# A two-layer decoder trunk on one core: a hand-written ScalarE order at three seams, weight casts placed behind the last turned block, and a different order inside a turned block

## The chip, the cores and the metric

The kernel runs on one core of one Trainium2 chip. The metric is device microseconds (us) of one execution, the median of several runs. The engines are named as the profile names them: PE is the matrix engine and PEld its weight loads, DVE is VectorE, ACT is ScalarE, POOL is GpSimd, SP is the engine that issues most of the DMAs. Results of PE land in eight PSUM banks, called `banks` in the rows; everything else lies in SBUF.

## The reference, cut to what matters

The trunk has a retention layer, then a native-sparse-attention (NSA) layer, and each is followed by a SwiGLU FFN. Every sub-layer is wrapped in two RMS norms: its output is normalised and added to the stream `h`, and the sum is normalised again on its way into the next sub-layer.

```
def rms_norm(x, g):
    y = x * rsqrt(mean(x * x, axis=-1) + 1e-6)
    return y * g
def swiglu_ffn(x, w_in, w_out):
    gate, up = split(x @ w_in, 2)
    return (silu(gate) * up) @ w_out
# x: 512 tokens of 1024 values, float32
h = h + rms_norm(sublayer(rms_norm(h, g_pre)), g_post)      # four times
```

The place where one sub-layer ends and the next begins is called a **seam** here: the last product of the one, both norms, and the first products of the next. There are three: A (retention to FFN 0, near 395 to 456 us), B (FFN 0 to NSA, near 765 to 829 us) and C (NSA to FFN 1, near 1085 to 1151 us).

## The kernel before

**Products.** Float32 accuracy is made from three products of a reduced type: `mm3` (lines 246 to 251) multiplies high by high (L249), high by low (L250) and low by high (L251), for operands that stand as a pair of a rounded high part and the rest. A weight tile is fetched by a DMA that SP issues (L225) into one of three `raw` buffers, ACT makes its high part (L237), and DVE subtracts that from the raw tile to make the low part (L240). Regular weights go through two buffers of each part (`whi`, `wlo`); weights that are kept for longer lie in slots of a pool and read `r` in the rows.

**A seam.** `out_stage` computes the sub-layer's output with tokens on the partitions, in two halves of 512 columns and four blocks of 128 tokens. `evac` takes a bank: ACT squares it with a running sum (L417), DVE multiplies it by the gain row (L418). `norm` (L345 to L364) serves one half of the tokens, p = 0 or 1: DVE makes an inverse root in a chain of small steps from L354 on, adds to `h` (L358), ACT squares with a sum (L359), DVE makes the second root, and the result is scaled into `t`, one block by ACT (L363), one by DVE (L364). Then the tokens must lie along the free axis again: `turn(p, kp)` transposes four 128x128 pieces on PE into one bank (L373), and for each of its two k ACT writes the high part (L376) and DVE the low part (L377). At seam B, where the turned stream is also wanted in plain form, ACT copies each of the two (L383).

**Products inside the seam.** `lead` fetches six weight tiles of the next sub-layer ahead of time. `prods` multiplies them with the first half of the tokens while the second half is still being normed, and `rest` with the second half once it is turned. `low(j)` is the DVE step for the low part of such a tile. So PE goes through these steps: the last product of the sub-layer, with the transposes of the first half in the middle of it; 144 products of 256 columns (six tiles, eight k, three each) with three more blocks of transposes among them; then four blocks of transposes of the second half and again 144 products of 256 columns; then the next sub-layer's regular products of 512 columns.

**What sets the order.** The program's order within an engine is chosen by a scheduler, except within a block where it is fixed by hand as the code is written:

```
with self.tc.manual_schedule(engines={E.PE, E.DVE}):
```

In `out_stage` that covers PE and DVE; ACT's place for each cast and each high part is the scheduler's. `more()` fetches as many of the six tiles as the pool has room for, whenever it is called. The NSA stage runs by a planner's list with its own `stream` of weights (high part at L1228, low part at L1232).

## Time and profile before

| what | value |
| --- | --- |
| median of three runs | 1488.17 us (1487.72 to 1488.86) |
| the profiled execution, own time | 1486.86 us |
| its span in the trace | 1485.1 us |
| PE busy | 1459.6 us, 98% of the span |
| ACT busy | 600.6 us, 40% |
| DVE busy | 732.1 us, 49% |
| granted PE clock, mean | 0.998 of full speed |

The profiled execution takes 1.76 us more than its span, and 1.31 us less than the median of the runs. Matrix products are pipelined in the trace, so that the next one starts before the end of the one ahead of it is shown: the distance from start to start is what a product costs, and a bracket behind a row gives the time the engine stood idle ahead of that row and the engine and tile that released it.

### The profile page before, as it was taken

Reading aid. Unit: us, or ns where it says so; the run is one execution under the profiler, and the core shown is the slowest. Engines: PE = TensorE matmul, PEld = TensorE weight load, DVE = VectorE, ACT = ScalarE, POOL = GpSimd, SP = SyncE. Lnnn points to the kernel's source line nnn. Section 1 sums busy time; section 2 is a strip of 40 time slices with the busy share of each in tenths; the row PEclk is TensorE's granted clock in tenths of the full one; section 3 lists DMA queues with packets and bytes.
Section 4 is the critical chain, followed back from the end, with each engine's and each line's share of the span. In section 5 each row is a group of like instructions: output and inputs, shape, how many; then the busy total and the mean of one; then the engine's idle time right before and its main releaser. Section 6 shows DMA issues by size and latency. Waiting matters only on the chain.

```text
span 1485.1 us, 18650 instructions
## 1 busy us (share of the span) xinstructions
PE 1459.6 (98%) x7286; PEld 1232.6 (83%) x7286; DVE 732.1 (49%) x1315; ACT 600.6 (40%) x1050; POOL 249.9 (17%) x369
## 2 busy tenths in 40 slices
PE   8999999999999999999998999999999999999997
PEld 6888888888888888888887988888889888888886
DVE  7546464734463333332346637888755333333244
ACT  5334333333442332222236348988753233322130
POOL 1012130402000000000000748787300000000000
PEclk9999999999999999999999999999999999999999
DMA  5223222325332344332243351321331222333231
GB/s 209 71 78 98 80 86 78 100 74 171 115 99 86 119 134 140 117 99 97 96 150 119 114 176 51 93 82 48 100 100 58 84 91 95 114 99 99 95 119 57
DMA packets 47833, 151.87 MB, mean 102 GB/s; under 512 B 5744, under 2 KB 6384, under 8 KB 47744
## 3 DMA queue, kind: packets, MB, share of 16 engines
q1 hardware_dynamic: 46560, 147.47, 31.2%
q10 hardware_dynamic: 1152, 3.15, 0.6%
q8 instruction: 57, 0.93, 0.3%
q14 instruction: 32, 0.26, 0.1%
q0 software_dynamic: 32, 0.07, 0.0%
HBM read 141.22 MB, written 9.44 MB: 101 GB/s over the span
## 4 chain that ended last, share of the span: by engine, by line
PE 92%; DVE 4%; DMA 2%; ACT 2%; issue 1%; SPq 0%; DVEq 0%; ACTq 0%
PE banks L250 27%; PE banks L249 27%; PE banks L251 27%; PE banks L1533 2%; PE banks L1555 1%; PE banks L1467 1%; PE banks L1468 1%; PE banks L1554 1%; DMA raw<-in_ffn_w_in_dram 1%; PE banks L1046 1%; DMA raw<-in_kv_w_n_dram 1%; DVE r L240 1%; PE banks L1365 1%; DVE r L1544 0%; ACT f L359 0%
## 5 line engine op out<-in xcount | busy, mean ns | idle before, releaser
L237 ACT ACTIVATE whi<-raw 128x1024 fp32r<-128x1024 f32 x165 | 174.7, 1059 | 518.8 <-PE banks L250 335.8
L249 PE MATMUL banks<-r,whi 128*128 128x512 f32 x912 | 357.4, 392 | 0.0
L251 PE MATMUL banks<-r,wlo 128*128 128x512 f32 x912 | 356.4, 391 | 0.0
L250 PE MATMUL banks<-r,whi 128*128 128x512 f32 x912 | 355.3, 390 | 0.0
L240 DVE TENSOR_TENSOR wlo<-raw,whi 128x1024 fp32r<-128x1024 f32 x165 | 206.0, 1249 | 299.2 <-ACT whi L237 295.2
L250 PE MATMUL banks<-r 128*128 128x256 f32 (+2 forms) x600 | 198.4, 334 | 5.0 <-DVE r L377 4.2
L250 PE MATMUL banks<-wlo,r 128*128 128x512 f32 x520 | 202.9, 390 | 0.0
L251 PE MATMUL banks<-whi,r 128*128 128x512 f32 x520 | 202.6, 390 | 0.0
L249 PE MATMUL banks<-r 128*128 128x256 f32 (+2 forms) x600 | 194.4, 333 | 8.0 <-ACT r L208 5.7
L251 PEld LDWEIGHTS banks<-r,wlo 128*128 128x128 f32 x912 | 171.2, 188 | 36.3 <-DVE f L678 0.7
L249 PEld LDWEIGHTS banks<-r,whi 128*128 128x128 f32 x912 | 171.3, 188 | 34.8 <-issue 0.9
L250 PEld LDWEIGHTS banks<-r,whi 128*128 128x128 f32 x912 | 171.3, 188 | 34.3
L251 PE MATMUL banks<-r 128*128 128x256 f32 (+2 forms) x600 | 195.3, 329 | 0.0
L249 PE MATMUL banks<-whi,r 128*128 128x512 f32 x520 | 178.5, 390 | 0.0
L250 PEld LDWEIGHTS banks<-r 128*128 128x128 f32 x600 | 114.1, 190 | 18.7 <-DVE r L377 8.0
L249 PEld LDWEIGHTS banks<-r 128*128 128x128 f32 x600 | 112.0, 191 | 20.7 <-ACT r L208 5.7
L251 PEld LDWEIGHTS banks<-r 128*128 128x128 f32 x600 | 114.2, 191 | 10.1 <-DVE r L209 0.2
L251 PEld LDWEIGHTS banks<-whi,r 128*128 128x128 f32 x520 | 97.6, 188 | 20.3 <-issue 0.2
L250 PEld LDWEIGHTS banks<-wlo,r 128*128 128x128 f32 x520 | 97.7, 188 | 20.2 <-issue 0.2
L249 PEld LDWEIGHTS banks<-whi,r 128*128 128x128 f32 x520 | 97.7, 188 | 20.0
L575 DVE TENSOR_TENSOR f<-banks,f 128x512 f32<-128x512 f32 x44 | 30.4, 692 | 137.7 <-PE banks L251 133.5
L949 POOL TENSOR_TENSOR r<-f,r 64x512 fp32r<-64x512 f32 x8 | 10.9, 1366 | 490.2 <-ACT r L942 489.8
(180 smaller groups left out, 1703.2 us busy)
## 6 DMA issues: line engine op xcount, KB each, us to landing
raw<-in_ffn_w_in_dram SPq DMA_DIRECT2D x88, 512.0 KB, 3.6
raw<-in_ffn_w_out_dram SPq DMA_DIRECT2D x44, 512.0 KB, 3.3
raw<-in_ret_w_g_dram SPq DMA_DIRECT2D x16, 512.0 KB, 3.6
raw<-in_ret_w_v_dram SPq DMA_DIRECT2D x16, 512.0 KB, 3.7
raw<-in_ret_w_out_dram SPq DMA_DIRECT2D x16, 512.0 KB, 3.8
f<-rows SPq DMA_DIRECT2D x32, 256.0 KB, 2.7
raw<-in_ret_w_qk_dram SPq DMA_DIRECT2D x12, 512.0 KB, 3.5
rows<-f SPq DMA_DIRECT2D x16, 320.0 KB, 4.4
```

Source lines behind the costliest of these rows:

```text
L237: self.nc.scalar.activation(hi[:, :n], raw[:, :n], AF.Copy)
L240: self.nc.vector.tensor_tensor(lo[:, :n], raw[:, :n], hi[:, :n].bitcast(F32), op=OP.subtract)
L249: t.matmul(out, shi, mhi, start=start, stop=False)
L250: t.matmul(out, shi, mlo, start=False, stop=False)
L251: t.matmul(out, slo, mhi, start=False, stop=stop)
L575: nc.vector.tensor_tensor(u.ap, pu, t.ap, op=OP.mult)
L1046: nc.tensor.matmul(ph[:, :NG * NCMP], box["w1", which, m, c][:, j * P:(j + 1) * P], box["xv", which][:, c * 8 + j].rearrange("p g n -> p ( ...
L1365: nc.tensor.matmul(st[2], self.kz[:, c:c + P], q[r].ap, start=r + i == 0, stop=r + i == 4)
L1467: nc.tensor.matmul(ps, qb, kh[:, ks, :w], start=True, stop=False)
L1468: nc.tensor.matmul(ps, qb, kl[:, ks, :w], start=False, stop=True)
L1533: nc.tensor.transpose(bank[2][:, c:c + P], probs[br][b][:, kb * P:(kb + 1) * P], self.ident)
L1554: nc.tensor.matmul(po[:, kb * P:], v, p.hi[:, c0:c0 + w], start=j == 0, stop=False)
```

## The change

It does five things.

1. The hand-written order at a seam covers ACT too, and `more()` becomes `fetch()`, which fetches one of the six tiles at a fixed place in the code.
2. `mark` and `behind`: the next two high parts of regular weights are issued after the last turned block of the seam.
3. `turn` writes its two high parts first, then at seam B one copy of 128x2x256 in the place of two of 128x256, and then the two low parts.
4. ACT's squares in `evac` are written to a common slot `junk`, no longer over the `t` block that DVE writes.
5. At seam B the plain copies lie in pairs, and the NSA stage frees them after each odd k. Some places of `low` and of the tail's products move.

```diff
+    def behind(self):
+        ins, n = self.mark
+        self.mark = ins, n - 1
+        return self.tc.issue_after(ins) if n > 0 else nullcontext()
...
-        self.nc.scalar.activation(hi[:, :n], raw[:, :n], AF.Copy)
+        with self.behind():
+            self.nc.scalar.activation(hi[:, :n], raw[:, :n], AF.Copy)
...
-        for i, k in enumerate(ks):
-            src, x = bank[:, i * 256:(i + 1) * 256], st["x"][k]
-            nc.scalar.activation(x.hi[:, cs], src, AF.Copy, scale=self.gain(gain, k))
+        srcs = [bank[:, i * 256:(i + 1) * 256] for i in range(2)]
+        for src, k in zip(srcs, ks):
+            last = nc.scalar.activation(st["x"][k].hi[:, cs], src, AF.Copy, scale=self.gain(gain, k))
+        if plain:
+            if p == 0:
+                st["n"].append(self.F.take(2))
+            last = nc.scalar.activation(st["n"][kp].ap.rearrange("p (a t) -> p a t", a=2)[:, :, cs],
+                                        bank.rearrange("p (a t) -> p a t", a=2), AF.Copy)
+        for src, k in zip(srcs, ks):
+            x = st["x"][k]
             nc.vector.scalar_tensor_tensor(x.lo[:, cs], src, self.gain(gain, k), x.hi[:, cs].bitcast(F32),
                                            op0=OP.mult, op1=OP.subtract)
-        if plain:
-            for i, k in enumerate(ks):
-                if p == 0:
-                    st["n"].append(self.F.take())
-                nc.scalar.activation(st["n"][k][:, cs], bank[:, i * 256:(i + 1) * 256], AF.Copy)
+        return last
...
-            nc.scalar.activation(t[b][:, cs], bank[c][b], AF.Square, accum_out=sq[:, c, b:b + 1])
+            nc.scalar.activation(junk.ap, bank[c][b], AF.Square, accum_out=sq[:, c, b:b + 1])
...
-        with self.tc.manual_schedule(engines={E.PE, E.DVE}):
+        with self.tc.manual_schedule(engines={E.PE, E.DVE, E.Activation}):
...
-                more()
...
+                second(tail.pop(0))
+            fetch()
+            fetch()
             self.norm(h, t, sq, pre[0], 0, lambda: low(1))
...
-            for i in tail[2:-1]:
+            for i in tail[:-1]:
                 second(i)
+            fetch()
             low(2)
-            low(3)
+            if not begun:
+                low(3)
             second(tail[-1], lambda: turn(0, 0))
...
-                if kp == 1:
+                if kp == 1 or kp == 2:
+                    fetch()
+                if kp == 1 and begun:
+                    low(3)
+                if kp == 2:
                     low(4)
...
             for kp in range(KT // 2):
-                turn(1, kp)
+                last = turn(1, kp)
             for b in (2, 3):
                 t[b].free()
+        self.mark = last.ins, 2
...
-        def more():
-            while len(ws) < len(tiles) and self.R.fits((2, 2)):
-                ws.append(self.chunk(src, tiles[len(ws)], KT, 0, base=base, keep=LATER))
+        def fetch():
+            ws.append(self.chunk(src, tiles[len(ws)], KT, 0, base=base, keep=LATER))
```

The order of ACT at seam A before, from the first half's norm to the last high part of that half (`r<-raw` and `whi<-raw` are casts of weights, `r<-banks,gains` the high parts of turned blocks, L363 the scale of `norm`, L417 the squares):

```order
L237 ACTIVATE r<-raw_2881 128x1024
L363 ACTIVATE f<-f,y_2863 128x1024
L376 ACTIVATE r<-banks,gains 128x256
L417 ACTIVATE f,sq_2289<-banks 128x512 x2
L376 ACTIVATE r<-banks,gains 128x256 x2
L237 ACTIVATE r<-raw_2884 128x1024
L237 ACTIVATE whi_3354<-raw_3352 128x1024
L376 ACTIVATE r<-banks,gains 128x256 x4
L237 ACTIVATE whi_3385<-raw_3383 128x1024
L376 ACTIVATE r<-banks,gains 128x256
```

The same stretch of ACT after the change, and from "..." on the second half's eight high parts with what follows them (the scale is L371 now, the high parts L384, the casts L245, the squares L429):

```order
L371 ACTIVATE f<-f,y_2848 128x1024
L245 ACTIVATE r<-raw_2890 128x1024
L384 ACTIVATE r<-banks,gains 128x256 x2
L429 ACTIVATE f,sq_2289<-banks 128x512 x2
L384 ACTIVATE r<-banks,gains 128x256 x2
L245 ACTIVATE r<-raw_2927 128x1024
...
L384 ACTIVATE r<-banks,gains 128x256 x8
L245 ACTIVATE whi_3354<-raw_3352 128x1024
L245 ACTIVATE whi_3385<-raw_3383 128x1024
```

A cast that stood ahead of the scale stands behind it now, and the two `whi` casts that stood among the first half's high parts stand behind those of the second half.

The order of DVE over the same stretch of seam A before (L377 are the low parts of turned blocks, L240 those of weights):

```order
L240 TENSOR_TENSOR r<-raw_2810,r 128x1024
L377 SCALAR_TENSOR_TENSOR r<-banks,gains,r 128x256 x2
L418 TENSOR_TENSOR f<-banks,f 128x512 x2
L377 SCALAR_TENSOR_TENSOR r<-banks,gains,r 128x256
L240 TENSOR_TENSOR wlo_3355<-raw_3352,whi_3354 128x1024
L377 SCALAR_TENSOR_TENSOR r<-banks,gains,r 128x256
L240 TENSOR_TENSOR r<-raw_2881,r 128x1024
L377 SCALAR_TENSOR_TENSOR r<-banks,gains,r 128x256 x3
L240 TENSOR_TENSOR wlo_3386<-raw_3383,whi_3385 128x1024
```

And after the change (L392 are the low parts of turned blocks, L248 those of weights):

```order
L248 TENSOR_TENSOR r<-raw_2890,r 128x1024
L392 SCALAR_TENSOR_TENSOR r<-banks,gains,r 128x256 x2
L430 TENSOR_TENSOR f<-banks,f 128x512 x2
L392 SCALAR_TENSOR_TENSOR r<-banks,gains,r 128x256 x4
L248 TENSOR_TENSOR r<-raw_2927,r 128x1024
L392 SCALAR_TENSOR_TENSOR r<-banks,gains,r 128x256 x2
```

The two `wlo` steps are gone from among the low parts of the first half, and they follow the second half's in the full list.

The order of ACT at seam B, second half of the tokens, before (L383 are the plain copies):

```order
L363 ACTIVATE f<-f,y_5498 128x1024
L376 ACTIVATE r<-banks,gains 128x256 x3
L383 ACTIVATE f<-banks 128x256 x2
L376 ACTIVATE r<-banks,gains 128x256 x2
L383 ACTIVATE f<-banks 128x256 x2
```

And after the change (L388 is the wide copy, L1251 the high part in the NSA stage's weight stream):

```order
L371 ACTIVATE f<-f,y_5494 128x1024
L384 ACTIVATE r<-banks,gains 128x256 x2
L388 ACTIVATE f<-banks 128x2x256
...
L388 ACTIVATE f<-banks 128x2x256
L1251 ACTIVATE whi_5672<-raw_5644 128x1024
L1251 ACTIVATE whi_5700<-raw_5646 128x1024
```

Each block is now two high parts and one wide copy, and two casts of the stream follow the last one.

## Rows read from the trace of the kernel before

**Rows 1.** Page, busy us (share of the span) and instructions of each engine.

```profile
PE 1459.6 (98%) x7286; PEld 1232.6 (83%) x7286; DVE 732.1 (49%) x1315; ACT 600.6 (40%) x1050; POOL 249.9 (17%) x369
```

**Rows 2.** Waits of PE, whole span: us in total, times, longest.

```profile
PE banks L250 <- DVE r L377: 4.2, 6, 1.0
PE banks L249 <- ACT r L376: 1.8, 3, 0.9
PE banks L373 <- ACT f L363: 1.3, 2, 0.7
```

**Rows 3.** Windows: length, busy of PE, PEld, DVE, ACT, POOL; clock, DMA, GB/s.

```profile
412.86:436.01 23.15, 21.60 (x167) 20.46 (x168) 16.58 (x42) 11.02 (x20) 0.00 (x0) 1.00 0.44 137
781.53:806.24 24.71, 21.92 (x167) 20.40 (x166) 17.38 (x44) 13.99 (x29) 0.00 (x0) 1.00 0.51 171
806.24:828.92 22.68, 21.75 (x162) 19.67 (x161) 13.29 (x22) 12.45 (x26) 12.27 (x10) 1.00 0.00 1
1106.69:1130.93 24.24, 21.85 (x167) 20.51 (x168) 17.57 (x43) 11.15 (x20) 0.00 (x0) 1.00 0.41 130
1130.93:1150.33 19.40, 19.27 (x163) 19.03 (x162) 6.46 (x12) 7.99 (x14) 0.00 (x0) 1.00 0.01 2
```

**Rows 4.** Timeline of PE at seams A and C: start, us, what, [idle before <- releaser].

```profile
411.69 0.39 PE L250 MATMUL banks<-r 128*128 128x512 f32 x1
411.92 0.39 PE L251 MATMUL banks<-r 128*128 128x512 f32 x1
412.86 0.66 PE L373 MATMUL banks<-ident,f 128*128 128x128 f32 x4 [0.56 <-ACT f L363]
413.27 0.49 PE L249 MATMUL banks<-r 128*128 128x512 f32 x1
...
419.46 0.38 PE L249 MATMUL banks<-r 128*128 128x256 f32 x1
420.39 0.38 PE L250 MATMUL banks<-r 128*128 128x256 f32 x1 [0.54 <-DVE r L377]
...
1105.55 0.39 PE L251 MATMUL banks<-r 128*128 128x512 f32 x1
1106.69 0.66 PE L373 MATMUL banks<-ident,f 128*128 128x128 f32 x4 [0.75 <-ACT f L363]
```

**Rows 5.** Timeline of ACT, seam A's first half and the same cast at seam C.

```profile
410.71 1.06 ACT L237 ACTIVATE r<-raw 128x1024 fp32r<-128x1024 f32 x1 [2.61 <-DMA raw<-in_ffn_w_in_dram]
411.68 1.13 ACT L363 ACTIVATE f<-f,y 128x1024 f32<-128x1024 f32 x1
...
417.62 1.06 ACT L237 ACTIVATE whi<-raw 128x1024 fp32r<-128x1024 f32 x1 [0.30 <-DMA raw<-in_ffn_w_in_dram]
...
421.90 0.84 ACT L376 ACTIVATE r<-banks,gains 128x256 fp32r<-128x256 f32 x2 [2.48 <-DVE r L377]
...
1104.54 1.06 ACT L237 ACTIVATE r<-raw 128x1024 fp32r<-128x1024 f32 x1 [2.79 <-DMA raw<-in_ffn_w_in_dram]
```

**Rows 6.** Groups by form, ACT and DVE: count, busy us, mean ns, idle before.

```profile
L377 DVE SCALAR_TENSOR_TENSOR r<-banks,gains,r 128x256 fp32r<-128x256 f32 x48 | 22.6, 481 | 25.5 <-ACT r L376 25.5
L1540 ACT ACTIVATE r<-banks 128x512 fp32r<-128x512 f32 x80 | 46.9, 590 | 11.5 <-PE banks L1533 9.8 <-DVE f L1575 0.9
```

**Rows 7.** Timeline of ACT and DVE at seam B, second half of the tokens.

```profile
806.88 1.50 ACT L376 ACTIVATE r<-banks,gains 128x256 fp32r<-128x256 f32 x3 [1.24 <-PE banks L373]
...
813.64 0.48 DVE L377 SCALAR_TENSOR_TENSOR r<-banks,gains,r 128x256 fp32r<-128x256 f32 x1 [0.54 <-ACT r L376]
```

**Rows 8.** Timeline of DVE and ACT at seam A, second half's norm, first and last.

```profile
426.18 0.15 DVE L354 SCALAR_TENSOR_TENSOR ms<-sq,pre 128x2 f32<-128x2 f32 x1
...
434.26 1.15 ACT L363 ACTIVATE f<-f,y 128x1024 f32<-128x1024 f32 x1 [2.27 <-DVE y L279]
```

**Rows 9.** Chain of waits around seam B: start, us, what.

```profile
782.72 4.60 DMA raw<-in_kv_w_n_dram
```

**Rows 10.** Waits of all engines at the start of the NSA stage, 845 to 925 us.

```profile
POOL r L949 <- ACT r L942: 25.5, 1, 25.5
```

More of the change, by code (lines that the diff above doesn't have):

```diff
@@ L1 @@
 from collections import deque
-from contextlib import ExitStack
+from contextlib import ExitStack, nullcontext
 import numpy as np
@@ L180, in __init__ @@
         self.n = 0
+        self.mark = None, 0
         nc = self.nc
@@ L462, in out_stage @@
                     (nc.sync, nc.scalar)[c].dma_start(self.a["out"][b][:, cs], h[b][:, cs])
+            junk.free()
+            row.free()
             return
@@ L477, in out_stage @@
                     low(0)
-            if begun:
-                mm(0, begun, defer, (2, 3))
-                defer.free()
-                more()
             def second(i, inside=None):
@@ L486, in second @@
                 free(i)
-                more()
             tail = sorted(kept)
-            for i in tail[:2]:
-                second(i)
+            if begun:
+                mm(0, begun, defer, (2, 3))
+                defer.free()
+            else:
+                second(tail.pop(0))
+            fetch()
+            fetch()
             self.norm(h, t, sq, pre[0], 0, lambda: low(1))
@@ L503, in out_stage @@
             row.free()
+            junk.free()
             for kp in range(1, KT // 2 + 1):
@@ L549, in prods @@
                      k == 0, k == KT - 1)
-        return tiles, more, ws, prods
+        return tiles, fetch, ws, prods
     def ffn_lead(self, l):
@@ L835, in nsa @@
             nc.sync.dma_start(self.pe[i], a["cmp_pe"][i])
-        o, begun, held = self.attend(st["n"], st, fin[1], w2t)
+        o, begun, held = self.attend([t[:, i * S:(i + 1) * S] for t in st["n"] for i in range(2)], st, fin[1], w2t)
         for t in held:
@@ L1227, in hi @@
             box["lo"] = self.wp.tile([P, 1024], F32R, name=self.nm("wlo"), tag="wlo", bufs=SPL)
-            nc.scalar.activation(box["hi"][:, :n], box["raw"][:, :n], AF.Copy)
+            with self.behind():
+                nc.scalar.activation(box["hi"][:, :n], box["raw"][:, :n], AF.Copy)
         def lo(i):
```

11 lines of the change are left out of this document (7 added, 4 removed).

## The prediction

> **What bounds the kernel now.** The page's busy times come first: PE is busy for 98% of the span and the next engine, DVE, for 49% [rows 1]. The change takes no product away, so all that it can win is time in which PE doesn't start a product though it has one left. Next come PE's waits. Those that the change touches are waits for the low part of a turned block, for its high part, and for the norm's scale [rows 2]; they add up to 7.3 us, all at the seams. The waits view shows only idle time, though, and a pipelined product that starts late is partly drawn as busy. So the third view is the table of windows, one for each half of each seam [rows 3], where the distance between fixed points of PE's programme counts.
>
> The second half of seam C is the cleanest of them: 19.40 us for 144 products of 256 columns and four blocks of transposes [rows 3]. With 0.4 us for a block (412.86 to 413.27, [rows 4]) and 0.1 us more behind it, that is 2 us for the blocks and 17.4 / 144 = 0.12 us for a product. The first half of a seam has the same, plus six products of 512 columns at 0.23 us from start to start (411.69 to 411.92, [rows 4]), 1.4 us. Undisturbed it would take 20.8 us. It takes 23.15 at A, 24.71 at B, 24.24 at C [rows 3], so it loses **2.35, 3.9 and 3.45 us**. The second half at B loses 22.68 - 19.40 = 3.3 us. Also the first transposes start late: 0.71 us at A (due at 411.92 + 0.23, started at 412.86) and 0.91 us at C [rows 4]. In all some 15 us are there to be won: 1%.
>
> The timeline of ACT tells why [rows 5]. At 410.71 ACT casts a weight tile for which it has stood 2.61 us waiting for the DMA; the norm's scale, on which the transposes hang, is behind it in ACT's queue and starts at 411.68. At C the same wait is 2.79 us. At 417.62 it again waits for a landing and casts a regular weight that PE needs only 39 us later, with high parts of turned blocks behind it. And at 421.90 two high parts have waited 2.48 us for DVE's low part of the block before: ACT and DVE take turns on one bank. PE sees it as a product that starts 0.93 us behind its neighbour (419.46 to 420.39, [rows 4]).
>
> **The change part by part.**
>
> *ACT's order fixed.* The cast that stood ahead of the scale now stands behind it. The scale is then only bound by DVE's root, and the first transposes lose their lateness: 0.71 us at A, 0.91 at C, none at B. What the cast waits for is its own tile, used by `prods` of a later tile.
>
> *Two regular casts behind the last turned block, high parts ahead of low parts.* The casts and their low parts leave the first half (per cast 1.06 us on ACT [rows 5], a little more on DVE). With both high parts in a row, a block costs ACT 0.84 us (the row at 421.90, [rows 5]), then DVE two lows of 0.48 us [rows 6]. From the transposes' start ACT needs 0.64 us to begin (806.24 to 806.88, [rows 3, 7]), so the first low is ready 0.64 + 0.84 + 0.48 = 1.96 us after it and the block is done at 2.4 us. A block is followed by 18 products, 2.2 us plus the transposes' 0.5 us, and the engines are a block ahead, so nothing in the first half should wait: A gains 2.35, C 3.45, B 3.9 us, less what follows.
>
> At B the wide copy stands between the high parts and the lows. It isn't in the trace; two copies of half the size in a row, or one pass of 128x512 out of a bank at 0.59 us [rows 6], bound it at 0.59 to 0.76; I take 0.6, as it is one instruction over the same columns. The block's first low then comes at 2.55 us. PE wants it after the transposes, the six 512-column products and the next block's transposes, 0.4 + 1.4 + 0.5 = 2.3 us: 0.2 us lost (0 to 0.4). B's first half gains 3.7.
>
> At C two evacuations now come ahead of the first low part on DVE: 0 to 0.5 us new, I take 0.25. In the second halves of A and C the low is ready at 1.96 us and PE wants it after two blocks of transposes and six products, some 1.1 + 6 x 0.12 = 1.8 us: 0.1 to 0.2 us lost each, I take 0.15.
>
> *Second half of B.* Four blocks go through the same two or three engines as fast as they can, and PE has too few products in between. Now the last low starts at 813.64 [rows 7] and ends 7.9 us after the transposes began. After the change ACT needs 0.64 us, then four times 0.84 + 0.6, then DVE two lows: 0.64 + 5.76 + 0.96 = 7.35 us. Neighbouring ACT instructions overlap by some 0.1 us, which would make it 6.85. The gain is 0.55 to 1.05 us; I take 0.85.
>
> Here a rule of the Trainium skill speaks against the wide copy. The page "PSUM — Partial Sum Buffer", section "PSUM bank collisions raise a hardware error", has it that two engines may not touch the same bank and quadrant of partitions at once, two reads included, and that a dependency is set between them. The trace agrees in that ACT's high part of a block waits 2.48 us for DVE's low part of its other half [rows 5]. By the rule the lows wait until the wide copy is through, as counted above; if it did not hold, the lows would run beside the copy, which is the third rival below.
>
> *What is late next.* The second half's norm takes from 426.18 to 434.26 + 1.15, 9.2 us [rows 8], and begins when DVE has done the last low of the first half. At A that low would be done near 421.8, the norm at 431.0, and PE gets to the transposes at 412.15 + 20.8 = 432.95. That leaves 1.9 us; 1.5 at B by the same sum with 0.6 more per block, and 2 at C. So the norm stays hidden, but not by far. The regular weights held back: two casts at 1.06 us behind the last high part are done some 9 us after the second half's start, PE wants them 20 us after it.
>
> *After B.* The stream's two casts and their lows go behind the turned blocks, so that DVE copies keys some 2 us later in PE's terms and POOL, which works from these, starts later. POOL then stands 25.5 us for ACT once [rows 10], so this is covered many times over: nothing. The common slot of the squares and the paired plain copies move no step that waits.
>
> **The sum.** A: 0.71 + 2.35 - 0.15 = 2.9. B: 3.7 + 0.85 = 4.55. C: 0.91 + 3.45 - 0.25 - 0.15 = 3.95. Together 11.4 us, of some 15. The profiled execution would take 1486.86 - 11.4 = 1475.5; the median of the runs lies 1.3 us above it, so the median is forecast at **1476.8 us**, 0.8% less. With the bounds of the terms (0.4 and 0.55 at B, 0.5 at C, 0.2 at A and C) it is 10.5 to 12.3 us; for what the sums by hand overlook I give the forecast case 8.5 to 13 us, 1475.2 to 1479.7.
>
> **The rivals.**
>
> 1. *The norm takes the place of the waits.* If DVE's last low of the first half comes 3 to 4 us later than counted, because a weight tile's low waits ahead of it for its cast, the 9.2 us norm ends after PE has got to the transposes, and 1.5 to 2 us are lost at each seam, 5.5 us in all: 1482.3. For it: the slack is only 1.5 to 2 us. Against: the norm itself starts some 4.4 us earlier at A than now (421.8 against 426.18).
>
> 2. *Slower: ACT stands for a landing, with the high parts behind it.* The fixed order has two casts of led tiles among the first half's turned blocks. A tile's landing took 4.60 us at B [rows 9], and its raw buffer comes free only with a DVE low. Today such waits last 2.61 and 2.79 us ahead of the scale [rows 5]. If both casts of each seam wait 2.7 us and PE feels it in full, that is 3 x 2 x 2.7 = 16.2 us: 16.2 - 11.4 = 4.8 us slower, 1493.0. It turns the sign once the six casts are on average 1.9 us late in PE's terms. Against: by the places of the fetches in the changed code, laid over the windows, a landing has some 11 us to spare at A, 5 at B and 1 at C (estimates).
>
> 3. *The lows run beside the copy at B.* Then the bank is passed on 0.6 us earlier in each of two rounds of the second half, 1.2 us, and the 0.2 us of the first half vanish: so the gain is 12.8 us and the median 1475.4. For it: the two only read the bank. Against: the wait of 2.48 us.
>
> 4. *No change.* The steps moved were hidden already and PE's lateness at the seams comes back, as when each seam's product order costs again what its waits did. It would take 11 of 15 us to stay: 1488.2. The order listing shows the casts moved, and the waits name just them.
>
> **How the numbers follow.** Forecast 0.65; rival 1 0.17; rival 2 0.05; rival 3 0.08; no change 0.05. The likeliest gives 1476.8. The range 1473.5 to 1482.5 takes the forecast case and rival 3 with the runs' spread and some 1.7 us for a gain closer to the 15 us, and half of rival 1: about 0.81. A measurement can tell 0.2% (3 us) from no change, so faster is 0.90 (forecast, rivals 1 and 3), same 0.05, slower 0.05.
>
> **What would show it.** Right: waits of PE for high and low parts near zero at A and C; the windows from first to second transposes 20.8 to 21.3 us; the first transposes 0.23 us behind the product before them at A and C; B's second half 21.5 to 22. Rival 1: idle time of PE ahead of the second half's first transposes, released by the scale. Rival 2: ACT idle behind a DMA with a high part next, and PE waiting for it. Wrong beyond that: time given back in the NSA stage, whose windows should keep their length.

## The result and the profile after

The changed kernel takes **1475.48 us** (median of four runs, 1474.87 to 1476.02) against 1487.97 us for the kernel before in the same comparison. The ratio is 0.9912 with a 95% interval of 0.990 to 0.9924: 12.5 us or 0.84% faster. The forecast was 1476.8 us and a gain of 11.4 us.

The profiled execution took 1476.02 us with a span of 1474.2 us, 10.9 us less than the span of before. The page's busy times [rows 1], and PE's waits at the seams [rows 2], now read:

```profile
PE 1455.2 (99%) x7286; PEld 1231.9 (84%) x7286; DVE 732.7 (50%) x1315; ACT 596.6 (40%) x1042; POOL 250.3 (17%) x369
```

```profile
PE banks L258 <- DVE r L392: 1.5, 3, 1.0
PE banks L1068 <- DMA raw<-in_cmp_w_dram: 0.8, 1, 0.8
```

The 4.2 us for low parts of turned blocks are down to 1.5, the waits for high parts (1.8 us) and for the norm's scale (1.3 us) are gone, and a wait of 0.8 us has come that the trace of before did not have, for a weight of the compression in the NSA stage. The windows that answer to [rows 3], from first to second transposes and from there to the first regular product, for A, B and C in turn (length, busy time of PE, PEld, DVE, ACT, POOL, clock, DMA share, GB/s):

```profile
413.27:433.65 20.38, 20.38 (x168) 20.08 (x166) 14.54 (x40) 9.86 (x19) 0.00 (x0) 1.00 0.34 104
433.65:454.28 20.63, 20.50 (x167) 19.82 (x166) 9.43 (x16) 8.09 (x15) 0.00 (x0) 1.00 0.27 84
779.35:799.98 20.63, 20.63 (x168) 20.14 (x167) 14.52 (x40) 11.70 (x23) 0.00 (x0) 1.00 0.46 154
799.98:821.91 21.93, 20.26 (x163) 19.33 (x161) 15.43 (x26) 13.36 (x24) 10.40 (x9) 1.00 0.14 49
1099.37:1119.86 20.49, 20.49 (x167) 20.15 (x166) 16.63 (x44) 10.71 (x21) 0.00 (x0) 1.00 0.33 103
1119.86:1139.43 19.57, 19.44 (x162) 19.09 (x161) 8.54 (x14) 9.37 (x16) 0.00 (x0) 1.00 0.19 55
```

The first halves went from 23.15, 24.71 and 24.24 us to 20.38, 20.63 and 20.49: 2.77 + 4.08 + 3.75 = 10.6 us. B's second half went from 22.68 to 21.93. The whole account of the span, from fixed point to fixed point of PE's programme, is this (us):

| stretch | before | after | difference |
| --- | --- | --- | --- |
| start to when A's first transposes are due | 412.15 | 413.27 | +1.12 |
| lateness of the first transposes, A and C | 0.71 + 0.91 | 0 + 0 | -1.62 |
| first halves A, B, C | 72.10 | 61.50 | -10.60 |
| second half B | 22.68 | 21.93 | -0.75 |
| second halves A and C | 39.85 | 40.20 | +0.35 |
| A's end to B's first transposes | 325.07 | 325.07 | 0 |
| B's end to C's first transposes, without lateness | 276.86 | 277.46 | +0.60 |
| C's end to the end | 334.8 | 334.8 | 0.0 |

The seams gave 12.6 us, the NSA stage took 0.6 us back, and the start of the program cost 1.1 us more in this execution. The start is not the change's doing, as far as the traces show: the last section gives how it varies from execution to execution. The median gained 12.5.

The first transposes now follow the product before them by 0.23 us, which answers to [rows 4]; at A and at C (start, us, what):

```profile
413.04 0.39 PE L259 MATMUL banks<-r 128*128 128x512 f32 x1
413.27 0.60 PE L381 MATMUL banks<-ident,f 128*128 128x128 f32 x4
...
1099.14 0.39 PE L259 MATMUL banks<-r 128*128 128x512 f32 x1
1099.37 0.60 PE L381 MATMUL banks<-ident,f 128*128 128x128 f32 x4
```

And ACT at seam A, which answers to [rows 5]:

```profile
410.75 1.15 ACT L371 ACTIVATE f<-f,y 128x1024 f32<-128x1024 f32 x1 [2.26 <-DVE y L287]
411.81 1.04 ACT L245 ACTIVATE r<-raw 128x1024 fp32r<-128x1024 f32 x1
...
418.31 0.84 ACT L384 ACTIVATE r<-banks,gains 128x256 fp32r<-128x256 f32 x2 [0.60 <-PE banks L381]
...
420.90 0.84 ACT L384 ACTIVATE r<-banks,gains 128x256 fp32r<-128x256 f32 x2 [0.80 <-PE banks L381]
```

The scale (410.75) waits for DVE's root alone, with the cast behind it; the high parts wait for PE's transposes and no longer for DVE's low part (2.48 us in [rows 5]). ACT has no wait for a landing left in any of the three seams.

### The profile page after: what moved, and what is told of

It reads as the page before. It is cut to its first block, busy times and chain, and to the rows that moved or that the text cites. A ratio compares the mean times of both kernels' runs of the same rounds, so it can differ in the third digit from the quotient of the medians.

```text
span 1474.2 us, 18710 instructions
## 1 busy us (share of the span) xinstructions
PE 1455.2 (99%) x7286; PEld 1231.9 (84%) x7286; DVE 732.7 (50%) x1315; ACT 596.6 (40%) x1042; POOL 250.3 (17%) x369
## 4 chain that ended last, share of the span: by engine, by line
PE 97%; DVE 1%; ACT 1%; DMA 1%; issue 0%; SPq 0%; DVEq 0%; ACTq 0%
PE banks L258 29%; PE banks L257 29%; PE banks L259 29%; PE banks L1556 2%; PE banks L1578 1%; PE banks L1490 1%; PE banks L1491 1%; PE banks L1577 1%; PE banks L1068 1%; PE banks L381 1%; PE banks L1388 1%; PE banks L300 0%; DMA f<-in_xT_dram 0%; PE banks L325 0%; DMA raw<-in_cmp_w_dram 0%; PE banks L1038 0%
## 5 line engine op out<-in xcount | busy, mean ns | idle before, releaser
L245 ACT ACTIVATE whi<-raw 128x1024 fp32r<-128x1024 f32 x165 | 174.4, 1059 | 515.0 <-PE banks L258 327.7
L248 DVE TENSOR_TENSOR wlo<-raw,whi 128x1024 fp32r<-128x1024 f32 x165 | 205.7, 1248 | 294.6 <-ACT whi L245 290.7
L971 POOL TENSOR_TENSOR r<-f,r 64x512 fp32r<-64x512 f32 x8 | 10.9, 1366 | 482.6 <-ACT r L964 482.2
```

Source lines behind the costliest of these rows:

```text
L245: self.nc.scalar.activation(hi[:, :n], raw[:, :n], AF.Copy)
L248: self.nc.vector.tensor_tensor(lo[:, :n], raw[:, :n], hi[:, :n].bitcast(F32), op=OP.subtract)
```

## The experiments

Each kernel is one or two edits away from the kernel before or the changed kernel. Since a median moves by a tenth of a per cent from chip to chip, the readings rest on the windows. Those of the seams repeat within 0.07 us where nothing in them changed; that of the NSA stage does not: the two traces of the changed kernel differ by 0.6 us in it. In one table (us; lateness of the first transposes at A and C; then the first halves, B's second half, and B's end to C's first transposes without lateness):

| kernel | late A, C | first A | first B | first C | second B | NSA | median (before beside it) |
| --- | --- | --- | --- | --- | --- | --- | --- |
| before | 0.71, 0.91 | 23.15 | 24.71 | 24.24 | 22.68 | 276.9 | 1487.97 |
| changed | 0, 0 | 20.38 | 20.63 | 20.49 | 21.93 | 277.5 | 1475.48 (1487.97) |
| changed, a second time | 0, 0 | 20.38 | 20.64 | 20.49 | 21.92 | 278.1 | 1475.76 (1488.46) |
| nothing held back | 0, 0 | 21.86 | 22.62 | 22.03 | 21.99 | 276.9 | 1480.19 (1488.79) |
| old block order | 0, 0 | 20.38 | 23.70 | 21.18 | 26.73 | 277.6 | 1482.96 (1488.79) |
| ACT left free | 0.85, 1.08 | 20.45 | 21.07 | 20.45 | 21.93 | 278.2 | 1478.10 (1488.79) |
| block order alone | 0.83, 0.93 | 20.73 | 21.84 | 21.81 | 21.25 | 277.7 | 1478.96 (1488.79) |
| held-back casts alone | 0.85, 0.85 | 21.27 | 21.39 | 21.71 | 22.67 | 281.2 | 1483.97 (1488.46) |
| nothing held back at B | 0, 0 | 20.38 | 23.32 | 20.49 | 21.99 | 276.9 | 1476.60 (1487.49) |

### Nothing held back

```diff
-        self.mark = last.ins, 2
+        self.mark = last.ins, 0
```

> The changed kernel with nothing held back: the number of weight casts placed behind the last turned block is 0 in the place of 2. The ScalarE order of the seam and the new order inside a turned block stay. Theory (the held-back casts are a part of the gain of their own): two casts of 1.06 us stand again among the high parts of the first half at A, and one of them may wait 0.3 to 0.8 us for its landing, with two low parts of 1.2 us among DVE's lows; PE loses 0.5 to 1 us at each seam, 1.5 to 3 us in all, so 1477 to 1478.5 us. Rival (the block order alone takes the waits away): no wait of PE for a high or low part at A and C, within 0.5 us of the changed kernel's 1475.5.

Measured: 1480.19 us, 0.9943 of before (0.9928 to 0.9958). The first halves lose 1.48, 1.99 and 1.54 us against the changed kernel, 5.0 in all. PE waits there for low parts, but also for the second half's scale, 1.8 us in three waits. At A (PE, start, us, what, [idle before <- releaser]) and ahead of it on DVE:

```profile
433.95 1.09 PE L381 MATMUL banks<-ident,f 128*128 128x128 f32 x8 [0.57 <-ACT f L371]
```

```profile
424.50 1.22 DVE L248 TENSOR_TENSOR wlo<-raw,whi 128x1024 fp32r<-128x1024 f32 x1 [1.25 <-ACT whi L245]
```

A weight's low part, which DVE has to wait 1.25 us for, stands within the norm's chain of small steps (the chain began at 422.31 and goes on behind it), so the scale starts 10.4 us after the chain began and not 8.1 as in the changed kernel, and PE arrives before it. This is the first rival's outcome by a near relative of its mechanism: a weight's low part that waits for its cast makes the norm late, though here it stands within the norm and not ahead of it. What keeps it out of the changed kernel is that the casts are held back. The theory held; its size, 1.5 to 3 us, was too small.

### The old order inside a turned block

```diff
         for src, k in zip(srcs, ks):
-            last = nc.scalar.activation(st["x"][k].hi[:, cs], src, AF.Copy, scale=self.gain(gain, k))
+            x = st["x"][k]
+            last = nc.scalar.activation(x.hi[:, cs], src, AF.Copy, scale=self.gain(gain, k))
+            nc.vector.scalar_tensor_tensor(x.lo[:, cs], src, self.gain(gain, k), x.hi[:, cs].bitcast(F32),
+                                           op0=OP.mult, op1=OP.subtract)
...
+            for i, src in enumerate(srcs):
+                last = nc.scalar.activation(st["n"][kp].ap[:, i * S + cs.start:i * S + cs.stop], src, AF.Copy)
```

> The changed kernel with the old order inside a turned block: high, low, high, low, then at B two narrow plain copies. Theory (ACT and DVE take turns on one bank): a block again costs ACT and DVE about 0.4 us more in a chain, which in the first halves is hidden for the most part by a block's 18 products (2.2 us) and costs 0 to 0.5 us a seam; at B's second half nothing hides it and 0.8 us come back, so 1476 to 1478. Rival (the block order is the main cause of the first halves' gain): the first halves of A, B and C lose 2 to 3 us each again, 1482 to 1485.

Measured: 1482.96 us, which lies in the rival's range, but not by its account: A's first half does not notice (20.38), C's loses 0.7, but B's halves lose 3.1 and 4.8 us. With ACT's order fixed, the copies of a block stand ahead of the next block's high parts, and ACT and DVE wait for each other at nearly every step (ACT at B's second half):

```profile
805.22 0.48 ACT L385 ACTIVATE r<-banks,gains 128x256 fp32r<-128x256 f32 x1 [0.55 <-DVE r L386]
806.25 0.66 ACT L392 ACTIVATE f<-banks 128x256 f32<-128x256 f32 x2 [0.55 <-DVE r L386]
```

The kernel before had the same block order, but there the scheduler let the next high part go ahead, and its second half took 22.68 and not 26.73. So at B the fixed order of ACT is only worth having with the new block order. A part of the 4.8 us is the clock (last section); the shares of the two are not measured.

### ACT's order left to the scheduler

```diff
-        with self.tc.manual_schedule(engines={E.PE, E.DVE, E.Activation}):
+        with self.tc.manual_schedule(engines={E.PE, E.DVE}):
```

> The changed kernel with ACT's order inside the seam left to the scheduler (PE and DVE fixed by hand as in the kernel before); the held-back casts and the new block order stay. In this build two casts of led weights stand ahead of the norm's scale at A again. Theory: the first transposes start 0.7 to 2 us late at A and C, and nothing else changes, so 1477 to 1479.5. Rival (the fixed order of ACT does nothing by itself): first transposes 0.23 us behind the product before, 1475.5.

Measured: 1478.10 us. The first transposes are late again by 0.85 and 1.08 us, and B's first half loses 0.44; A's and C's don't move. The theory held, but for B's first half. With the other two parts in place the fixed order is worth the lateness, 1.6 to 1.9 us, and little else.

### The new block order alone

```diff
         for i, k in enumerate(ks):
             src, x = bank[:, i * 256:(i + 1) * 256], st["x"][k]
             nc.scalar.activation(x.hi[:, cs], src, AF.Copy, scale=self.gain(gain, k))
+        for i, k in enumerate(ks):
+            src, x = bank[:, i * 256:(i + 1) * 256], st["x"][k]
             nc.vector.scalar_tensor_tensor(x.lo[:, cs], src, self.gain(gain, k), x.hi[:, cs].bitcast(F32),
                                            op0=OP.mult, op1=OP.subtract)
```

> The kernel before with one edit: inside a turned block the two high parts come first, then the two low parts, then at B the two narrow copies. Theory (three causes add): the scale stays late (1.6 us in all) and regular casts stay among the high parts; a part of the first halves' 10.5 us is won, so 3 to 6 us less than before, 1482 to 1485. Rival 1 (the block order is nearly all): 1478 to 1479. Rival 2 (it does nothing without the held-back casts): within 1.5 us of before.

Measured: 1478.96 us (1477.8 to 1481.89), 9.8 us less than before on that chip and in the first rival's range, not the theory's. It takes 2.42, 2.87 and 2.43 us off the first halves, 7.7 of the 10.6, and 1.4 off B's second half, where the changed kernel wins only 0.75. ACT's rows at that place show what the scheduler makes of it:

```profile
802.78 1.57 ACT L376 ACTIVATE r<-banks,gains 128x256 fp32r<-128x256 f32 x4 [1.92 <-PE banks L373]
804.57 1.44 ACT L385 ACTIVATE f<-banks 128x256 f32<-128x256 f32 x4 [0.21 <-DVE r L379]
```

It takes two blocks at a time, four high parts and then four copies. So at B's second half the hand-written order with the wide copy ahead of the lows is 0.68 us slower than this one.

### The held-back casts alone

```diff
+        self.mark = last.ins, 2
...
+        with self.behind():
             self.nc.scalar.activation(hi[:, :n], raw[:, :n], AF.Copy)
```

> The kernel before with one edit: the next two casts of regular weights are issued behind the last turned block. ACT's order at the seam is otherwise the scheduler's, and the order inside a block is the old one. Theory (the parts overlap: the block order alone cut the first halves by 2.4, 2.9 and 2.4 us, holding back on top of the rest 1.5, 2.0 and 1.5 us): the first halves lose 1 to 2 us less than before at each seam, the scale stays late by 0.7 and 0.9 us, B's second half stays at 22.7; 3 to 6 us faster than before, 1482 to 1485. Rival (held-back casts are only worth something with the new block order): within 1.5 us of before.

Measured: 1483.97 us, 0.9968 of before (0.9957 to 0.998): 4.5 us faster, as the theory had it. But the first halves are 1.88, 3.32 and 2.53 us shorter than before, 7.7 us, more than was expected. The median hides it, since the NSA stage takes 281.2 us in this trace, 4.4 more than before: 3.06 us are a wait of PE for a weight, taken up below, and some 1.7 us a lower clock right behind that wait (last section). So either part alone wins 7.7 us in the first halves and both win 10.6: **the parts overlap**. At A the same products are seen to gain by either. In the kernel before, the products behind those at 419.46 and 425.13 start 0.93 and 1.18 us after them, where it is 0.12 after the change. Each waits for a low part of a turned block that stands on DVE behind a weight's low part; for the first of them the rows are

```profile
418.72 1.22 DVE L240 TENSOR_TENSOR wlo<-raw,whi 128x1024 fp32r<-128x1024 f32 x1 [0.60 <-ACT whi L237]
419.86 0.48 DVE L377 SCALAR_TENSOR_TENSOR r<-banks,gains,r 128x256 fp32r<-128x256 f32 x1
```

The block order alone brings both distances to 0.12 us, the held-back casts alone bring them to 0.47 and 0.12, so what one of the two takes away is no longer there for the other. At B and C this reading is carried over and not shown.

The fixed order of ACT, with the smaller edits that came with it, depends on the other two as well. Added to the block order alone it makes the first halves 2.1 us longer in all (64.4 to 66.5, the kernel with nothing held back); added to the held-back casts alone it gains 1.4 us at A and C and loses 2.3 at B (the kernel with the old block order); added to both it gains 0.5.

### The lows ahead of the wide copy

```diff
+        for src, k in zip(srcs, ks):
+            x = st["x"][k]
+            nc.vector.scalar_tensor_tensor(x.lo[:, cs], src, self.gain(gain, k), x.hi[:, cs].bitcast(F32),
+                                           op0=OP.mult, op1=OP.subtract)
         if plain:
...
             last = nc.scalar.activation(st["n"][kp].ap.rearrange("p (a t) -> p a t", a=2)[:, :, cs],
                                         bank.rearrange("p (a t) -> p a t", a=2), AF.Copy)
-        for src, k in zip(srcs, ks):
-            x = st["x"][k]
-            nc.vector.scalar_tensor_tensor(x.lo[:, cs], src, self.gain(gain, k), x.hi[:, cs].bitcast(F32),
-                                           op0=OP.mult, op1=OP.subtract)
```

> The changed kernel with one swap at seam B: the two low parts of a turned block come ahead of the wide plain copy. Theory (a bank serves one engine at a time, so whatever comes first delays the rest): the first low is ready 0.6 us earlier, PE's wait of 0.99 us at the start of B's second half shrinks to 0.3 to 0.5, but the bank is passed on to the third and fourth block no earlier, so B's second half goes from 21.93 to between 21.3 and 21.7 and its first half stays at 20.6; 1475 to 1475.3 by the clock of the first comparison. Rival (the lows run beside the copy anyway and the order between them says nothing): no difference in that window.

Measured: 1480.43 us, where better was expected. B's first half goes from 20.63 to 22.82, its second from 21.93 to 23.98. ACT in B's second half:

```profile
801.02 0.84 ACT L384 ACTIVATE r<-banks,gains 128x256 fp32r<-128x256 f32 x2 [1.92 <-PE banks L381]
802.80 0.60 ACT L392 ACTIVATE f<-banks 128x512 f32<-128x512 f32 x1 [0.94 <-DVE r L387]
803.29 0.83 ACT L384 ACTIVATE r<-banks,gains 128x256 fp32r<-128x256 f32 x2
805.07 0.60 ACT L392 ACTIVATE f<-banks 128x512 f32<-128x512 f32 x1 [0.94 <-DVE r L387]
```

The copy waits 0.94 us for the lows, once per block, and the next block's high parts stand behind it in ACT's queue. The expectation looked at the bank and forgot the queue. Its one part that came true is the smaller wait for a low part (0.5 us at most, 0.99 in the changed kernel). Both the theory's time and its rival fell.

### B's second half two blocks at a time

The transposes of two blocks, in two banks, come first, then this:

```diff
+        for kp, bank in blocks:
+            for i in range(2):
+                k = 2 * kp + i
+                nc.scalar.activation(st["x"][k].hi[:, cs], bank[:, i * 256:(i + 1) * 256], AF.Copy, scale=self.gain(gain, k))
+        for kp, bank in blocks:
+            for i in range(2):
+                k = 2 * kp + i
+                x = st["x"][k]
+                nc.vector.scalar_tensor_tensor(x.lo[:, cs], bank[:, i * 256:(i + 1) * 256], self.gain(gain, k), x.hi[:, cs].bitcast(F32),
+                                               op0=OP.mult, op1=OP.subtract)
+            last = nc.scalar.activation(st["n"][kp].ap.rearrange("p (a t) -> p a t", a=2)[:, :, cs],
+                                        bank.rearrange("p (a t) -> p a t", a=2), AF.Copy)
```

> The changed kernel with B's second half made two blocks at a time: four high parts in a row, then for each block its lows and its wide copy, so that ACT is on one bank while DVE is on the other. Theory: the first low is ready 0.64 + 0.84 + 0.48 = 1.96 us after the transposes began, the copies wait for the lows but no high part does, and B's second half falls from 21.93 to 20.6 to 21.2 us. Rival (ACT's total time sets that stretch, about 4 x 1.45 us): 21.7 to 22.

Measured: B's second half takes 21.26 us and not 21.93, just above what was expected (20.6 to 21.2 us), and what the scheduler reached with the block order alone (21.25). The copy still waits, but 0.2 us, since DVE works on one bank while ACT is on the other. The median was 1477.41 us, with runs from 1475.03 to 1479.48, no better than the changed kernel: in the trace, which is of the run at 1479.48, the NSA stage takes 280.88 us, with 2.5 us of PE's waiting for the compression's weight and some 1.6 us of a lower clock behind it (last section).

### Nothing held back at B

```diff
-        self.mark = last.ins, 2
+        self.mark = last.ins, 0 if keep is not None else 2
```

> The changed kernel with the two casts held back at A and C, and not at B. Theory: B's first half loses the 2.0 us that it lost with nothing held back (20.63 to 22.6), and the NSA stage, from B's end to C's first transposes, takes 276.9 us in the place of 277.46, without the wait for a weight of the compression (0.80 us in the changed kernel); 1476.9 us. Rival (that wait comes from something else than the casts behind the last block): the stage stays at 277.4 or above with the wait in it.

Measured: 1476.60 us. B's first half loses 2.69 us (2.0 expected). The NSA stage takes 276.87 us and the new wait is gone, as expected.

### The second half's norm made later

```diff
+            for _ in range(2):
+                nc.vector.tensor_tensor(t[0].ap, h[2].ap, h[3].ap, op=OP.subtract)
             for b in range(2):
                 t[b].free()
```

> The changed kernel with two DVE steps of 1024 columns (some 1.2 us each, 2.4 us) that serve nothing, ahead of the second half's norm at each seam. Theory (the norm is hidden by 1.96 us at A, 1.37 at B, 1.80 at C in the changed kernel's trace): the second half's first transposes are late by 0.45, 1.05 and 0.6 us, waiting for the scale of the norm; 2.1 us in all. Rival (the norm has more cover than these rows say): not late at all. Rival (it is on the path already): 7.2 us.

Measured: one execution, 1478.23 us. The first halves take 0.61, 1.09 and 0.65 us longer, against 0.45, 1.05 and 0.6 expected (A's cover is 1.85 us and not 1.96 by the exact start of the transposes, 433.65), and PE's waits name the scale:

```profile
PE banks L381 <- ACT f L371: 1.5, 3, 0.6
```

So the cover that the trace shows is real to a tenth of a microsecond. Three rows give it, the ends of the scale (start plus duration) being 431.80, 798.61 and 1118.06 against the transposes at 433.65, 799.98 and 1119.86:

```profile
430.65 1.15 ACT L371 ACTIVATE f<-f,y 128x1024 f32<-128x1024 f32 x1 [2.26 <-DVE y L287]
...
797.46 1.15 ACT L371 ACTIVATE f<-f,y 128x1024 f32<-128x1024 f32 x1 [2.26 <-DVE y L287]
...
1116.91 1.15 ACT L371 ACTIVATE f<-f,y 128x1024 f32<-128x1024 f32 x1 [2.26 <-DVE y L287]
```

### The keys ahead of the held weights' low parts

`late` is 3.2 for the two weights that are held back at B, and 0 for all others.

```diff
-            plan.at(t - 1.9 + i, "POOL" if pool else "DVE", 1.3 if pool else 0.6, ("x", "wlo", name, i), lambda i=i: lo(i), [("ACT", "whi", name)])
+            plan.at(t - 1.9 + i + late, "POOL" if pool else "DVE", 1.3 if pool else 0.6, ("x", "wlo", name, i), lambda i=i: lo(i), [("ACT", "whi", name)])
```

> The changed kernel with the low parts of the two held-back weights of seam B planned 3.2 us later, so that on DVE the first copy of the keys comes ahead of them. Theory (at B the held casts' low parts delay the keys by 1.9 us, POOL's work on them frees a slot later, SP's queue stands on that slot with a weight's DMA behind it, and PE waits 0.80 us for a weight of the compression): the wait is gone, the NSA stage takes 276.9 us in the place of 277.46, B's halves stay at 20.6 and 21.9; 0.6 us faster than the changed kernel on the same chip. Rival (that wait follows from PE's being earlier alone, whatever DVE does): the wait stays at 0.5 to 2 us.

Measured: 1475.41 us beside 1475.76 for the changed kernel on the same chip, with overlapping runs, so no difference can be claimed. The wait is 0.57 us and not gone, and the stage takes 277.27; beside 0.80 and 1.38 us in two traces of the changed kernel that would show little, but the DMA behind it is issued 0.56 us earlier (2.24 and 2.80, table below), where those two traces agree to 0.01. The theory named a part of the cause.

### Both, and the changed kernel again

The last edit together with the one that makes two blocks at a time, and the changed kernel unaltered beside them.

> Both edits on the changed kernel: B's second half two blocks at a time, and the keys' first copy ahead of the held weights' low parts. Theory: B's second half 21.26 us as in the run with the first edit alone, and the NSA stage back at 276.9 to 277.3, where that run took 280.9 with 2.5 us of waiting for the compression's weight; 1.1 to 1.3 us faster than the changed kernel on the same chip. Rival (what PE wins at B is given back at that weight, since its DMA is paced by POOL): NSA stage at 278 to 281, no faster than the changed kernel.

> The changed kernel once more, as the measure for the runs beside it on the same chip. Expected 1475.5 by all theories, with 20.4, 20.6 and 20.5 us for the first halves, 21.9 for B's second half and 277.5 from B's end to C's first transposes. If the wait for the compression's weight depends on the run, it may lie between 0 and 2 us here, against 0.80 in the first trace.

Measured: both edits 1474.73 us (1474.36 to 1475.28), the changed kernel 1475.76 (1474.59 to 1475.95), 0.9907 and 0.9912 of before. The windows say that B's second half stays at 21.25; the NSA stage takes 278.03 and 278.07 with waits of 1.33 and 1.38 us for the compression's weight, so the theory's 276.9 to 277.3 did not come, and the stage lies at the lower end of the rival's range. The medians differ by 1.0 us, the expected direction, but the runs overlap: a better kernel is likely and not shown.

## Why the prediction was right

**The bound and the places.** PE's lost starts at the seams were the whole of it: 12.6 us came from there, and the other stretches behind the first seam kept their length to 0.1 us but for the NSA stage. One reading on the way was off: the high part at 421.90 [rows 5] is said in one place to wait for the low part of the block before. By the order of the rows it is the low part of its own block's other half, as the text has it further on. And the product at 420.39, which is taken there as what PE sees of this, waits for the low part at 419.86, which stood behind a weight's low part on DVE (rows above): it belongs to the casts that are held back now.

**ACT's order.** Lateness 0.71 and 0.91 us was to go, and went. With ACT left to the scheduler it came back (0.85, 1.08). That the fixed order also lengthens or shortens the halves, by what stands beside it, was in no term of the sum.

**First halves.** 2.35, 3.7 and 3.2 us (with the new stalls) were forecast, 2.77, 4.08 and 3.75 came: 1.35 us more. The step that was mis-sized is the undisturbed time. It was taken as 20.8 us by way of C's second half, but the three first halves take 20.38 to 20.63, below the 20.8 to 21.3 named as the sign. That second half has a late start of its own in it, in the kernel before:

```profile
1130.93 1.04 PE L373 MATMUL banks<-ident,f 128*128 128x128 f32 x8
1132.09 0.98 PE L249 MATMUL banks<-r 128*128 128x256 f32 x6
```

The eighth transpose starts at 1131.69, so the first product stands 0.40 us behind it; in the first halves after the change that distance is 0.03. The stalls of 0.2 us at B and 0.25 us at C, which the sum took off, don't appear as waits; the windows leave 0.25 us at B and 0.11 at C above A's 20.38. The 0.15 us each that the sum took off for the second halves of A and C came as 0.18 and 0.17.

**Which part does it.** The prediction put the first halves' gain on two edits together and gave no shares. The runs show that shares don't add: 7.7 us for either alone, 10.6 for both.

**B's second half.** 0.85 us forecast, 0.75 measured, with the steps as counted; that another order wins 1.4 there (the block order alone) was not seen. The wide copy lasts 0.60 us, as taken, and the lows wait for it (ACT, DVE and PE at that place):

```profile
800.61 0.84 ACT L384 ACTIVATE r<-banks,gains 128x256 fp32r<-128x256 f32 x2 [2.00 <-PE banks L381]
801.34 0.60 ACT L388 ACTIVATE f<-banks 128x512 f32<-128x512 f32 x1
```

```profile
801.97 0.88 DVE L392 SCALAR_TENSOR_TENSOR r<-banks,gains,r 128x256 fp32r<-128x256 f32 x2 [3.82 <-ACT f L388]
```

```profile
802.51 0.39 PE L258 MATMUL banks<-r 128*128 128x256 f32 x1 [0.99 <-DVE r L392]
```

DVE is released by the copy, not by the high part that it needs, and PE waits 0.99 us for DVE. That is the rule of the Trainium skill, page "PSUM — Partial Sum Buffer", section "PSUM bank collisions raise a hardware error", at work: two readers of a bank are kept apart. With it the third rival falls.

**The norm's cover.** 1.9, 1.5 and 2 us were forecast; the trace has 1.85, 1.37 and 1.80, and the run with 2.4 us of extra work confirms them. The first rival didn't come about, but it was close: with nothing held back PE waits for the scale at all three seams, 1.8 us where the rival had 5.5.

**Slower.** The second rival needed ACT to stand for landings ahead of high parts. In none of the seams does ACT wait for a DMA now.

**What was wrong: "After B ... nothing".** The NSA stage lost 0.6 us in the first trace and 1.2 in the second. The prediction saw that the keys would come 2 us later in PE's terms, looked at POOL's one long wait of 25.5 us [rows 10], and took it as cover. The step that failed is this: POOL's lateness reaches PE by another way, SP's queue. In the changed kernel, SP, then PE:

```profile
840.65 0.32 SPq L842 DMA_DIRECT2D f<-rows  x1
841.06 0.38 SPq L232 DMA_DIRECT2D raw<-in_kv_w_t_dram  x1
```

```profile
SPq L842 <- POOL f L1138: 1.6, 1, 1.6
```

```profile
838.26 3.73 PE L1068 MATMUL banks<-f,raw 128*128 128x124 f32 x32
```

SP waits for a slot that POOL frees (L1138), with the DMA of a weight behind that wait. That weight's landing, cast and low part free the raw buffer for the compression's weight, and PE waits for this one. The DMA is issued 2.80 us after the compression's products began, and 1.97 us after it in the trace of before, where PE itself, and not POOL, released it. POOL frees the slot later in PE's terms: the `f<-rows` that SP issues into it comes 0.28 us after the products' start before, and 2.39 us after it in the changed kernel. Over all traces:

| kernel | DMA issued after those products began, us | it landed after they began, us | PE's wait, us |
| --- | --- | --- | --- |
| before; nothing held back; nothing held back at B | 1.97, 1.97, 1.98 | 6.6, 6.8, 6.8 | 0, 0, 0 |
| block order alone | 1.97 | 7.8 | 0.48 |
| keys first | 2.24 | 7.5 | 0.57 |
| changed, twice | 2.80, 2.81 | 7.6, 8.3 | 0.80, 1.38 |
| ACT free; norm late | 2.80, 2.81 | 8.4, 8.8 | 1.56, 2.02 |
| skew and keys first; old block order | 2.91, 2.96 | 8.2, 7.7 | 1.33, 0.87 |
| held-back casts alone | 3.93 | 9.4 | 3.06 |
| lows first; skew | 4.16, 4.17 | 8.4, 9.2 | 1.73, 2.52 |

("Skew" is B's second half two blocks at a time.) Every kernel that keeps the casts behind B's last block has the DMA late and a wait; of the four that don't, three have none. That the held casts bring the late issue is shown (without them at B alone it is gone). The wait goes with the landing: none up to 6.8 us, 0.5 to 0.9 at 7.5 to 7.8, 1.3 to 2.0 at 8.2 to 8.8, and 2.5 and 3.1 at 9.2 and 9.4. So of one kernel with the same issue, the wait differed (0.80 and 1.38) as the landing did; the cast that stands for it on ACT, in the two traces:

```profile
846.00 1.06 ACT L1251 ACTIVATE whi<-raw 128x1024 fp32r<-128x1024 f32 x1 [3.56 <-DMA raw<-in_kv_w_t_dram]
```

```profile
845.98 1.06 ACT L1251 ACTIVATE whi<-raw 128x1024 fp32r<-128x1024 f32 x1 [4.20 <-DMA raw<-in_kv_w_t_dram]
```

The products began at 838.26 and 837.61, so the cast starts 7.74 and 8.37 us after them. In the same way the block order alone, with the DMA on time, has a wait because the landing took 5.9 us. What makes a landing take 4.2 us in one trace and 6.0 in another, and what else than the low parts delays POOL, stays open: moving the low parts behind the keys took back only 0.56 of the 0.83 us of lateness.

**The sum.** Part of its closeness is luck. The first halves gave 1.35 us more than forecast, and the NSA stage, put at nothing, took 0.6 to 1.2 us back.

## What to carry to other kernels

Where two engines take turns on a bank, let one finish its steps on it before the other begins, and let nothing that waits for a DMA stand in that engine's queue; but expect two such edits to overlap, so that their separate gains (7.7 us each here) add to less (10.6). A fixed order can hurt with the wrong neighbours: with the old block order the fixed order of ACT made B's second half 4.0 us longer than the scheduler's (26.73 and 22.68 us, the clock included), and with the block order alone the scheduler beat it there too (21.25 and 21.93). So compare a hand-written order with the scheduler's at each place. And when an edit makes one engine later in terms of another, follow it through every queue that stands behind a resource it frees, SP's too, before calling it covered.

## What the runs showed of the hardware that was not expected

The clock: in the run with the old block order, PE's granted clock fell in B's second half. PE had just been starting products with gaps (15 in 3 us, then 13, where 27 fit), and four windows from there on read:

```profile
801.00:804.00 3.00, 2.60 (x15) 1.72 (x13) 0.97 (x2) 1.31 (x4) 0.00 (x0) 1.00 0.00 1
804.00:807.00 3.00, 2.70 (x13) 1.86 (x11) 0.97 (x2) 1.90 (x7) 0.00 (x0) 0.72 0.00 0
...
813.00:816.00 3.00, 3.00 (x18) 3.00 (x17) 2.91 (x5) 1.00 (x2) 0.00 (x0) 0.57 0.14 46
816.00:819.00 3.00, 3.00 (x27) 3.00 (x27) 0.88 (x2) 2.69 (x5) 2.01 (x2) 1.00 0.81 269
```

The mean granted clock goes to 0.72 and 0.57, a part of each window at the lower of the two levels. It falls twice, and the second time it is low while PE is fully busy again (813 to 816 us: 18 products in place of 27). In the kernel before, with 22.68 us for the same stretch, it stayed at 1.00. The same is seen in the NSA stage of the two kernels with the longest waits for the compression's weight: right behind PE's wait of 2.52 us (two blocks at a time) and of 3.06 us (held-back casts alone) the windows read

```profile
854.00:858.00 4.00, 4.00 (x19) 3.92 (x20) 0.00 (x0) 0.00 (x0) 0.00 (x0) 0.61 0.42 162
```

```profile
858.00:862.00 4.00, 4.00 (x17) 3.48 (x16) 0.00 (x0) 0.00 (x0) 0.00 (x0) 0.57 0.49 147
```

and the products in them take some 1.6 and 1.7 us more than the same ones next to them. The other traces, with waits of 0 to 2.02 us, stay at 1.00 there. So a wait can cost twice, once as a gap and once as clock.

The start: in all traces the first products of 512 columns begin 0.43 us apart and go over to 0.23 us at a point between 10.0 and 14.1 us into the span. The windows there show a granted clock of 1.00, but the trace holds no record of that clock ahead of this point (the first begins at 11.53 us before, at 13.69 in the changed kernel and at 11.58 in its second trace), so the 1.00 is no reading. The spacing is that of the lower level, as in the NSA stage of the kernel with the held-back casts alone, within the window of 0.57 above:

```profile
859.93 0.63 PE L258 MATMUL banks<-r,whi 128*128 128x512 f32 x1
860.36 0.63 PE L259 MATMUL banks<-r,wlo 128*128 128x512 f32 x1
```

A's first transposes started at 413.27 in the first trace of the changed kernel and at 412.63 in the second; over all traces they are due between 411.35 and 413.67. So profiled executions differ by up to 2.3 us from each other before the first seam, and 1.1 us of what the profiled gain (10.9) lacks to the median's (12.5) lie there. What sets that point the runs don't show.
